# The first layer's down projection as seven half-size products, with the weight sums computed in both layers

## The chip, the cores and the metric

One NeuronCore of a Trainium2 chip runs the whole kernel. The metric is the device time of one execution in microseconds (us), as the median of several executions. The engines are named as the profile names them: PE (TensorE, matmuls) with PEld (its weight loads), DVE (VectorE), ACT (ScalarE), POOL (GpSimd) and SP (SyncE, which only issues DMAs here).

## The reference

A decoder trunk of two layers over 512 tokens of width 1024, all float32. Each layer has a token mixer of three branches (an RWKV-7 recurrence, chunked retention, a spatial gate), merged by gates and added to `x`, and then a gated MLP with a causal convolution of width 3:

```
for l in range(DEPTH):                                  # DEPTH = 2
    h = rmsnorm(x, norm1_g[l])
    p = h @ w_in[l]
    ...                                                 # three branches, gates
    x = x + jnp.sum(gates * proj, axis=2) @ w_out[l]
    x = x + conv_ffn(rmsnorm(x, norm2_g[l]), ffn_w_up[l], ffn_conv_w[l], ffn_conv_b[l], ffn_w_down[l])
return rmsnorm(x, final_g)

def conv_ffn(h, w_up, conv_w, conv_b, w_down):
    u = h @ w_up                                        # 1024 -> 2 * 2816
    ...                                                 # causal conv of width 3
    gate, val = jnp.split(c, 2, axis=-1)
    return (jax.nn.silu(gate) * val) @ w_down           # 2816 -> 1024
```

The change concerns the last product, `(silu(gate) * val) @ w_down`: 2816 rows of weights are 22 blocks of 128, or 11 pairs of blocks, and there are 1024 output features and 512 tokens.

## The kernel before

**Products.** To keep float32 precision every matrix product is done as three passes (`mm3`, L146): both operands are split into a high part rounded to the matmul's format and the low remainder, and high x low, high x high and low x high are accumulated. A block of weights of 128 x 512 elements is called a unit. `unit` (L81) hands out units in the order in which they are used and keeps a few loaded and split ahead: `load` (L122) issues the DMA on SP, `part` (L131) makes the high part on ACT (L140) and the low part on DVE (L141). `AHEAD` says how many units are split ahead for each kind of stage.

**Layout.** Within a layer activations stand with features on the partitions and tokens along the free dimension. `act` is the MLP's inner activation.

**The up projection** (`ffn_up`, L1090) has 44 columns of 128 outputs: 22 gate columns (index `i`) and the value column that belongs to each. One column is two units, 24 matmuls of 128x512. For each column DVE multiplies by the norm's factor (`fu`, L1120), ACT starts the convolution (`cv`, L1122), DVE adds its other two taps (L1123, L1124); for each `i` ACT and DVE make the gated product `fth` (L1128, L1129). In the first layer each `fth` is then split (L1131). In the second layer two neighbours are combined by `halves` (L1140): four DVE operations on 128x256 halves, three DMAs to DRAM on POOL's queue, and two splits.

**The down projection of the first layer** (`ffn_down`, L1158) is plain: for each of 8 blocks of outputs `m`, 22 x 3 matmuls of 128x512 over `act`, with weights from `wdn`; then `x[m]` is updated (L1164), normalised for the next layer, squared, and stored by POOL (L1168).

**The down projection of the second layer** (`last`, L1173) is done by a scheme of Strassen's kind: each pair of weight blocks (256 rows) with the two halves of the outputs makes a 2 x 2 block matrix, the tokens' halves likewise, and seven products of half the size replace eight. Four of the seven weight operands are sums and differences of the raw blocks. They don't depend on the activations, and `presum` (L246) computes them early: four loads of raw blocks on POOL's queue (L262), four DVE operations of 128x512 (L251 to L254), four stores to DRAM on POOL's queue (L257). The table `PRE` (L27) places the 11 pairs: four in the first layer's up projection (at `i` = 2, 4, 6, 8), seven in the first layer's down projection (one for each `m` from 0 to 6).

**The recurrence** (`rwkv`, from L703) runs over 8 chunks `c` of 64 tokens. Its small matmuls wait for DVE and ACT (`xb`, printed as XB, L717; `U`, L731; the state `St`, printed as S, L742 and L743); while they wait, PE works at units of other projections (`fill`), with weights as `wh`, `wl` in three buffers. After every second chunk the output `y` is normalised (a power on POOL, L762), transposed on DVE (`yt`) and sent through DRAM and back (`turned`, L233: one store `tr`, four loads `yF`), on SP's queue.

**The norm between the layers** (`norm_bcast`, L285) sums the squares over the partitions by two 128x512 matmuls with a matrix of ones (L290, L291), inside the first columns of the next stage (`firstF`, L320).

DVE, ACT and POOL execute in the order in which their instructions stand. `keep_in_program_order` (`po`, `kept`) pins an instruction to its place among the other pinned ones of its engine; the rest is placed by a scheduler when the program is built.

## Time and profile before

| | |
|---|---|
| three executions | 1694.98, 1695.05, 1697.68 us; median 1695.05 |
| profiled execution | 1692.75 us; its span 1691.0 us, 1.75 us lie around it |
| granted TensorE clock | 0.999 |
| first layer: up projection, down projection | about 505 to 734 us, 734 to 853 us |
| second layer: up projection, down projection | about 1347 to 1583 us, 1583 to 1685 us |
| recurrences (8 chunks) | about 210 to 300 us, 1056 to 1145 us |
| POOL queue: `pre<-wdt` loads, `ts<-pre` stores | 44 of each, 256 KB each |
| SP queue: `wr<-wall`, `wr<-wdn`, `wr<-wdt`, `wr<-ts` | 480, 48 (8 of them half-size), 33, 44 |

The profile shows one execution, engine by engine. A group row gives a source line, its engine, its operation, its shapes and its count, with the busy time and the mean duration of one. Matmuls are pipelined: their durations overlap (a 128x512 matmul shows 390 ns), so what a matmul costs is read from the distance between the starts of two that follow each other. "Idle before" names what an engine waited for ahead of an instruction.

### The profile page before, as it was taken

What the parts mean: (1) busy time and instruction counts of PE and PEld (TensorE: products, weight loads), DVE (VectorE), ACT (ScalarE), POOL (GpSimd) and SP (SyncE); (2) the same over time, 40 slices, a digit from 0 to 9 for tenths busy, and PEclk for the clock granted to TensorE, in tenths of its full rate; (3) what the DMA queues carried; (4) which work ended last, traced back from release to release, by engine and by line L of the source; (5) the groups of instructions that cost most, each with busy time, mean ns of one, the idle gap of its engine ahead of it and who ended that gap; (6) DMA issues with size and microseconds to landing.
All of it is one profiled execution on the core that took longest, in us unless ns stands there. A gap on an engine that the chain in (4) does not pass through costs nothing.

```text
span 1691.0 us, 27937 instructions
## 1 busy us (share of the span) xinstructions
PE 1682.8 (100%) x10247; PEld 1382.6 (82%) x10247; DVE 1216.5 (72%) x2115; ACT 794.1 (47%) x1365; POOL 261.3 (15%) x376
## 2 busy tenths in 40 slices
PE   9999999999999999999999999999999999999998
PEld 7888877888888888888888888778888888888887
DVE  7887745578669877665568888465786688887877
ACT  6563533554255444433346544335542544444565
POOL 1121000303301200003321210003032012210000
PEclk9999999999999999999999999999999999999999
DMA  5236553625544533147743265536254424443775
GB/s 183 88 111 203 179 176 98 189 84 163 191 144 149 194 124 95 63 146 263 250 147 96 92 206 187 176 100 188 84 163 166 152 98 144 142 140 110 242 247 178
DMA packets 143385, 260.01 MB, mean 154 GB/s; under 512 B 19440, under 2 KB 35440, under 8 KB 143248
## 3 DMA queue, kind: packets, MB, share of 16 engines
q1 hardware_dynamic: 117056, 188.41, 35.5%
q0 software_dynamic: 17552, 54.15, 9.7%
q10 hardware_dynamic: 8640, 15.67, 2.6%
q8 instruction: 80, 1.31, 0.3%
q14 instruction: 57, 0.47, 0.1%
HBM read 212.94 MB, written 45.22 MB: 153 GB/s over the span
## 4 chain that ended last, share of the span: by engine, by line
PE 99%; DVE 1%; ACT 0%; DMA 0%; issue 0%; DVEq 0%; ACTq 0%
PE acc L157 89%; PE sm L157 3%; PE sm L694 2%; PE sm L948 1%; PE sm L601 1%; PE sm L1056 0%; PE acc L359 0%; PE sm L564 0%; PE sm L563 0%; PE sm L976 0%; PE sm L1003 0%; PE sm L848 0%; PE acc L319 0%; PE sm L839 0%; DMA wr<-wall 0%; PE sm L618 0%
## 5 line engine op out<-in xcount | busy, mean ns | idle before, releaser
L157 PE MATMUL acc<-lo,sh 128*128 128x512 f32 x1108 | 432.1, 390 | 0.0
L157 PE MATMUL acc<-hi,sh 128*128 128x512 f32 x1108 | 432.0, 390 | 0.0
L157 PE MATMUL acc<-hi,sl 128*128 128x512 f32 x1108 | 425.0, 390 | 0.0
L140 ACT CAST sh<-wr 128x512 fp32r<-128x512 f32 (+1 forms) x375 | 226.4, 614 | 294.7 <-PE acc L157 165.7
L141 DVE TENSOR_TENSOR sl<-wr,sh 128x512 fp32r<-128x512 f32 (+1 forms) x375 | 253.0, 683 | 95.3 <-ACT sh L140 70.2
L141 DVE TENSOR_TENSOR wl<-wr,wh 128x512 fp32r<-128x512 f32 x238 | 167.9, 708 | 142.8 <-ACT wh L140 139.9
L140 ACT CAST wh<-wr 128x512 fp32r<-128x512 f32 x238 | 146.9, 619 | 247.6 <-PE acc L157 155.6
L157 PEld LDWEIGHTS acc<-hi,sl 128*128 128x128 f32 x1108 | 208.0, 188 | 43.8 <-DVE gth L1071 0.3
L157 PEld LDWEIGHTS acc<-lo,sh 128*128 128x128 f32 x1108 | 208.1, 188 | 43.7 <-issue 0.9
L157 PEld LDWEIGHTS acc<-hi,sh 128*128 128x128 f32 x1108 | 208.0, 188 | 43.2 <-issue 0.3
L157 PE MATMUL acc<-lo,wh 128*128 128x512 f32 x584 | 230.1, 394 | 0.1
L157 PE MATMUL acc<-hi,wl 128*128 128x512 f32 x584 | 228.3, 391 | 0.0
L157 PE MATMUL acc<-hi,wh 128*128 128x512 f32 x584 | 227.7, 390 | 0.0
L1122 ACT ACTIVATE cv<-fu,pc 128x512 f32<-128x512 f32 x88 | 71.7, 816 | 139.4 <-DVE fu L1120 139.2
L157 PEld LDWEIGHTS acc<-hi,wl 128*128 128x128 f32 x584 | 109.6, 188 | 24.1 <-issue 0.9
L157 PEld LDWEIGHTS acc<-lo,wh 128*128 128x128 f32 x584 | 109.6, 188 | 23.8 <-DVE rwp L523 0.5
L157 PEld LDWEIGHTS acc<-hi,wh 128*128 128x128 f32 x584 | 109.7, 188 | 22.3 <-issue 0.2
L157 PE MATMUL acc<-ah,sh 128*128 128x512 f32 x352 | 108.3, 389 | 0.0
L1123 DVE SCALAR_TENSOR_TENSOR cv<-fu,pc,cv 128x511 f32<-128x511 f32 x88 | 65.8, 749 | 34.3 <-ACT cv L1122 34.3
L157 PE MATMUL acc<-wl,hi 128*128 128x512 f32 x212 | 85.8, 405 | 0.0
L1120 DVE TENSOR_TENSOR fu<-acc,rsF 128x512 f32<-128x512 f32 x88 | 60.3, 685 | 32.5 <-PE acc L157 31.5
L157 PE MATMUL acc<-wh,hi 128*128 128x512 f32 x212 | 82.5, 389 | 0.0
(368 smaller groups left out, 2452.5 us busy)
## 6 DMA issues: line engine op xcount, KB each, us to landing
wr<-wall SPq DMA_DIRECT2D x480, 256.0 KB, 2.9
gd<-gth ACTq DMA_DIRECT2D x48, 256.0 KB, 3.3
gth<-gd POOLq DMA_DIRECT2D x48, 256.0 KB, 3.3
pre<-wdt POOLq DMA_DIRECT2D x44, 256.0 KB, 6.0
ts<-pre POOLq DMA_DIRECT2D x44, 256.0 KB, 3.0
wr<-ts SPq DMA_DIRECT2D x44, 256.0 KB, 4.0
wr<-wdn SPq DMA_DIRECT2D x40, 256.0 KB, 3.7
wr<-wdt SPq DMA_DIRECT2D x33, 256.0 KB, 3.8
```

The lines of the kernel that those rows point to most:

```text
L140: self.kept(self.nc.scalar.copy(hi[:, :n], raw[:, :n]))
L141: self.kept(self.nc.vector.tensor_tensor(lo[:, :n], raw[:, :n], hi[:, :n], op=SUB))
L157: i = self.nc.tensor.matmul(*x, **y, **kw)
L601: i = T.matmul(pK[hv[1 - h], j, :], bk[hv[h], c, 1, :], x[hv[h], c, :], start=True, stop=True)
L694: po(T.matmul(o, l, r, start=start, stop=True, skip_group_check=True))
L948: po(T.matmul(X[h][:, i, :], lhsT, rhs, start=new[h], stop=stop, skip_group_check=True))
L1120: V.tensor_tensor(u, ps, self.rsF, op=MUL)
L1122: A.activation(t, u, AF.Identity, scale=self.p("cw2", j), bias=self.p("cb", j))
L1123: V.scalar_tensor_tensor(t[:, 1:], u[:, :511], self.p("cw1", j), t[:, 1:], op0=MUL, op1=ADD)
```

## The change

1. `ffn_down` uses seven products of half the size, as `last` does, but keeps features on the partitions: a unit of weights is 128 x 512 (half of the outputs), and each product multiplies 4 blocks of 128 outputs with 256 tokens. That is 11 pairs x 7 products x 4 blocks x 3 passes = 924 matmuls of 128x256, in place of 8 x 22 x 3 = 528 of 128x512. The code that both layers share moves to `kit` and `half`. Weights of both layers now come from `wdt` and the sums; `wdn` is gone.
2. `ffn_up` calls `halves` in the first layer too, and pins its order there from the third `i` on.
3. The weight sums are needed for both layers, and each layer makes its own: `sums_rw` makes four pairs (`RWS`) inside the layer's recurrence, in chunks 2 to 7, `sums` makes the other seven inside its up projection, one DVE operation ahead of each column for `i` from 3 to 16 (`UPS`). All these DVE operations and DMAs are pinned.
4. `norm_bcast` is replaced between the layers by `norm_stats` and `norm_rows`, which the first layer already used at its start: four 128x1 matmuls on the plain sum of squares, a power on POOL, four 128x128 transposes, a copy. They stand two half columns apart.
5. In the recurrence `xb` and `St` are pinned, and the trip of `y` through DRAM goes to POOL's queue.

```diff
-PRE = {(0, "f", 2): 0, (0, "f", 4): 1, (0, "f", 6): 2, (0, "f", 8): 3, (0, "d", 0): 4, (0, "d", 1): 5, (0, "d", 2): 6, (0, "d", 3): 7,
-       (0, "d", 4): 8, (0, "d", 5): 9, (0, "d", 6): 10}
+RWS, RWB, UPS = 4, (2, 4, 5, 6), range(3, 17)
-AHEAD = {None: 2, "p": 4, "r": 3, "f": 3, "u": 5, "q": 4}
+AHEAD = {None: 2, "p": 4, "r": 3, "f": 3, "u": 5, "q": 4, "k": 5, "w": 3}
...
+    def summed(self, l, q, b, p):
+        po = self.tc.keep_in_program_order
+        o, x, op = {7: (3, 1, SUB), 5: (1, 0, SUB), 6: (0, 3, ADD), 4: (2, 0, SUB)}[p]
+        po(self.nc.vector.tensor_tensor(b[o], b[o], b[x], op=op))
+        self.tsum[l, q, p] = self.dp.tile([128, 512], F32, name=self.nm("ts"))
+        po(self.nc.gpsimd.dma_start(self.tsum[l, q, p], b[o]))
...
+    def sums_rw(self, l):
...
+        first, b = [tile(0, 3, 1)], tile(0, 0, 2)
+        first.append(tile(1, 3, 1))
+        yield
+        for q in range(RWS):
+            b.update(first.pop(0))
+            self.summed(l, q, b, 7)
+            if q and q < RWS - 1:
+                first.append(tile(q + 1, 3, 1))
+            yield
+            for p in (5, 6, 4):
+                self.summed(l, q, b, p)
+            if q < RWS - 1:
+                b = tile(q + 1, 0, 2)
+            yield
+
+    def sums(self, l):
...
+        for q in range(RWS, NFF // 2):
+            n = get(q + 1) if q < NFF // 2 - 1 else None
+            for p in (7, 5, 6, 4):
+                self.summed(l, q, b, p)
+                yield
+            b = n
...
-                self.norm_bcast(st, l and ids[0] == 12)
+                self.norm_stats(st) if ids[0] == FIRST[0] else self.norm_bcast(st)
+            elif i == at + 2 and ids[0] == FIRST[0]:
+                self.norm_rows()
...
-            V.tensor_copy(xb, Q[:, 1])
+            po(V.tensor_copy(xb, Q[:, 1]))
+            self.presum(c - 1 in RWB)
...
-                    V.tensor_tensor(St, St, Q[:, 0], op=ADD)
+                    po(V.tensor_tensor(St, St, Q[:, 0], op=ADD))
                     po(V.tensor_tensor(St, St, f, op=MUL))
+                self.presum(c == 1 or c in RWB)
...
-            self.turned(o, self.r(n="yt"), y, nc.sync)
+            self.turned(o, self.r(n="yt"), y, nc.gpsimd)
...
-            self.keep = l == L - 1 and i > 1
+            self.keep = i > 1
             for j in (i, NFF + i):
+                self.presum(i in UPS)
...
-            if l < L - 1:
-                act.append(self.split(th, at))
-            elif i % 2 == 0:
+            if i % 2 == 0:
...
     def ffn_down(self, l, act, x, st):
-        for m in range(8):
-            ps = self.acc()
-            self.matF(ps, ("wdn", l, m, 0), act)
-            V.scalar_tensor_tensor(x[m], ps, 0.5, x[m], op0=MUL, op1=ADD)
+        def prod(ps, x, at, w, first, end, ms=range(4)):
+            for m in ms:
+                c = slice(128 * m, 128 * m + 128)
+                self.mm3(ps[m // 2][:, H[m % 2]], (w[0][:, c], w[1][:, c]), (x[0][:, at:at + 256], x[1][:, at:at + 256]),
+                         first and m % 2 == 0, end, skip_group_check=True)
...
+        for q in range(Q):
+            s, t = act[q][:2]
+            for p in (7, 5, 6, 4) if q < Q - 1 else (6, 7, 5, 4):
+                w = unit(p, q)
+                side(n)
+                n += 1
+                xs, at = {7: (t, 0), 5: (s, 0), 6: (s, 256), 4: (t, 256)}[p]
+                prod(pss[p], xs, at, w, q == 0, q == Q - 1)
...
+        for q in range(Q):
+            w = unit(1, q)
+            rest(q)
+            prod(out[1], ab[q], 0, w, False, q == Q - 1)
...
+        for q in range(Q):
+            w = unit(2, q)
+            prod(out[2], ab[q], 256, w, q == 0, q == Q - 1)
...
+        for q in range(Q - KEPT):
+            w = unit(3, q)
+            prod(out[3], s4[q // 2], q % 2 * 256, w, q == 0, False)
...
```

What moves is shown at three places. Line numbers of the changed program are its own (L140 and L156 there are L141 and L157 before). The first is PE where the first layer's down projection stands; `acc` is the accumulator in PSUM, behind the arrow stand the moving operand (`ah`, the split inner activation) and the weights. Before, this is a block of 128 outputs, here the head of the second of eight, which has 66 such rows:

```order
L157 MATMUL acc_1628_7673<-ah_1149_5568,sh_1612_7610 128x512
L157 MATMUL acc_1628_7673<-ah_1148_5567,sh_1612_7610 128x512
L157 MATMUL acc_1628_7673<-ah_1148_5567,sl_1613_7611 128x512
L157 MATMUL acc_1628_7673<-ah_1163_5624,sh_1612_7610 128x512
L157 MATMUL acc_1628_7673<-ah_1162_5623,sh_1612_7610 128x512
L157 MATMUL acc_1628_7673<-ah_1162_5623,sl_1613_7611 128x512
```

In the changed program this is the head of the first product, and such rows go on through 77 units of weights:

```order
L156 MATMUL acc_1694_7813<-ah_1186_5736,wh_1668_7706 128x256
L156 MATMUL acc_1694_7813<-ah_1185_5735,wh_1668_7706 128x256
L156 MATMUL acc_1694_7813<-ah_1185_5735,wl_1669_7707 128x256
L156 MATMUL acc_1694_7813<-ah_1186_5736,wh_1668_7706 128x256
L156 MATMUL acc_1694_7813<-ah_1185_5735,wh_1668_7706 128x256
L156 MATMUL acc_1694_7813<-ah_1185_5735,wl_1669_7707 128x256
L156 MATMUL acc_1695_7814<-ah_1186_5736,wh_1668_7706 128x256
```

A row after has half the tokens of a row before, and one unit of weights now serves 12 rows in a run, with four blocks of outputs side by side in two accumulators. The 528 rows of 128x512 (the first block among the last rows of the up projection) become 924 of 128x256. Outside of this stage PE's order is the same but for item 4 and for one fill unit in each layer that stands 45 rows earlier or later.

The second place is DVE at the last chunk (`c` = 7) of the first layer's recurrence; `wl` are the low parts of fill units, `ro` and `rb` belong to the rotary embedding. Before:

```order
L717 COPY XB_98_397<-sm_617_3329 128x256
L916 TENSOR_TENSOR ro_624_3422<-ro_624_3422,rb__625_3423 128x8x32
L141 TENSOR_TENSOR wl_632_3485<-wr_621_3404,wh_631_3484 128x512
L911 TENSOR_TENSOR ro_633_3500<-qs_589_3161,tab_577_3080 128x512
L912 TENSOR_TENSOR rb__634_3501<-qs_589_3161,tab_578_3081 128x8x32
L141 TENSOR_TENSOR wl_644_3539<-wr_627_3444,wh_643_3538 128x512
L753 TENSOR_REDUCE s1_635_3514<-y_607_3267 128x8
```

After, with the sums of the fourth pair (`cs` are their raw blocks, two blocks to a tile):

```order
L749 COPY XB_98_397<-sm_637_3389 128x256
L950 TENSOR_TENSOR ro_645_3485<-ro_645_3485,rb__646_3486 128x8x32
L140 TENSOR_TENSOR wl_656_3557<-wr_642_3467,wh_655_3556 128x512
L945 TENSOR_TENSOR ro_657_3572<-qs_603_3203,tab_585_3104 128x512
L946 TENSOR_TENSOR rb__658_3573<-qs_603_3203,tab_586_3105 128x8x32
L249 TENSOR_TENSOR cs_615_3289<-cs_615_3289,cs_631_3364 128x512
L140 TENSOR_TENSOR wl_668_3611<-wr_651_3516,wh_667_3610 128x512
L249 TENSOR_TENSOR cs_631_3364<-cs_631_3364,cs_615_3289 128x512
L249 TENSOR_TENSOR cs_631_3364<-cs_631_3364 128x512
L787 TENSOR_REDUCE s1_659_3586<-y_623_3315 128x8
```

A sum that reads `cs_631` now stands ahead of the fill unit's low part `wl_668`. The third place is POOL over chunks 5 to 7 of the same recurrence. Before it held two powers of the norm of `y` and then the trips of the rotary tiles:

```order
L762 TENSOR_TENSOR rs8_559_2957<-s2_558_2954,con_78 128x8
L762 TENSOR_TENSOR rs8_603_3255<-s2_602_3252,con_78 128x8
L243 DMA tr_700_3814<-qkt_699_3812 128x512
L239 DMA qkT_698_3811<-tr_700_3814 32x4x128 x4
L243 DMA tr_703_3823<-qkt_702_3821 128x512
```

After, the second of these powers is followed by the trip of `y` and the stores (`ts`) and loads of the sums:

```order
L251 DMA ts_614_3287<-cs_588_3129 128x512
L256 DMA cs_615_3289<-wdt 128x512 x2
L796 TENSOR_TENSOR rs8_619_3303<-s2_618_3300,con_78 128x8
L242 DMA tr_622_3309<-yt_621_3307 128x512
L238 DMA yF_620_3306<-tr_622_3309 32x4x128 x4
L251 DMA ts_628_3356<-cs_588_3129 128x512
L251 DMA ts_629_3359<-cs_596_3179 128x512
L251 DMA ts_630_3362<-cs_596_3179 128x512
L256 DMA cs_631_3364<-wdt 128x512 x2
```

The load of `cs_631` stands behind the four loads `yF`, which wait for the landing of `tr_622`, which waits for DVE's transpose of `y`.

More of the change, by code (lines that the diff above doesn't have):

```diff
@@ L265, in norm_new, with get, presum @@
+    def sums(self, l):
+        def get(q):
+            b = {i: self.f(n="pre") for i in (3, 1, 0, 2)}
+            self.raw4(l, q, b)
+            return b
+        b = get(RWS)
+        yield
[3 more added lines that the diff above has]
+                self.summed(l, q, b, p)
+                yield
+            b = n
+    def presum(self, ok=True):
+        if ok:
+            next(self.sum, None)
     def norm_new(self):
@@ L1102, in ffn_up @@
         first = self.firstF(l, (78, 79, 80), st, 3)
-        if l == 0:
-            self.fpre = [[self.f(n="pre") for _ in range(4)] for _ in range(4)]
+        self.sum = self.sums(l)
+        self.presum()
         for i in range(NFF):
-            if l == 0 and i % 2 == 0 and 2 <= i <= 10:
-                self.presum(l, "f", i)
             if x and i % 2 == 1 and i < 17:
@@ L1171, in ffn_down @@
+        self.pin = self.keep = False
         return x, xd
```

173 lines of the change are left out of this document (102 added, 71 removed).

## The prediction

> **What bounds the kernel now.** I read the page's busy times first, then its chain of work that ended last.
>
> ```profile
> PE 1682.8 (100%) x10247; PEld 1382.6 (82%) x10247; DVE 1216.5 (72%) x2115; ACT 794.1 (47%) x1365; POOL 261.3 (15%) x376
> ...
> PEclk9999999999999999999999999999999999999999
> ...
> PE 99%; DVE 1%; ACT 0%; DMA 0%; issue 0%; DVEq 0%; ACTq 0%
> ```
>
> PE is busy for 1682.8 of 1691.0 us at a granted clock of 0.9 or more in every slice, and the chain is PE's own work for 99%. So only fewer or cheaper PE rows can shorten the program, and everything that the change lays on other engines costs nothing until PE has to wait for it. The second view is a table of stretches: the first layer's up and down projection, the end of its recurrence, the second layer's up and down projection.
>
> ```profile
> core 0: us, PE busy (x) PEld busy (x) DVE busy (x) ACT busy (x) POOL busy (x), PEclk, DMA share, GB/s
> 505.00:745.00 240.00, 240.00 (x1060) 198.77 (x1060) 185.50 (x285) 114.19 (x176) 15.03 (x28) 1.00 0.38 123
> 745.00:865.00 120.00, 120.00 (x532) 99.36 (x530) 63.28 (x100) 40.37 (x69) 34.31 (x64) 1.00 0.73 242
> 200.00:300.00 100.00, 99.78 (x1416) 77.85 (x1415) 50.78 (x100) 40.63 (x78) 7.23 (x7) 1.00 0.45 139
> 1347.00:1583.00 236.00, 236.00 (x1043) 195.45 (x1042) 193.57 (x309) 106.40 (x174) 38.36 (x70) 1.00 0.41 131
> 1583.00:1685.00 102.00, 102.00 (x480) 85.09 (x478) 79.34 (x158) 60.35 (x115) 4.33 (x8) 1.00 0.71 235
> ```
>
> PE has no idle time in either projection and 0.22 us in 100 of the recurrence. DVE is loose in the down projection (63 of 120 us), tighter in the last stage (79 of 102), and nearest to its limit in the up projections.
>
> **The down projection.** The cost of a matmul is the distance between starts. The first two rows are the ends of a run of 47 rows of 128x512 in the last stage, the other two of a run of 36 rows of 128x256.
>
> ```profile
> 1659.68 0.39 PE L157 MATMUL acc<-sh,hi 128*128 128x512 f32 x1
> ...
> 1670.11 0.39 PE L157 MATMUL acc<-wh,lo 128*128 128x512 f32 x1
> ...
> 1680.78 0.28 PE L157 MATMUL acc<-sl,hi 128*128 128x256 f32 x1
> ...
> 1684.98 0.28 PE L157 MATMUL sm<-sh,lo 128*128 128x256 f32 x1
> ```
>
> 10.43 us over 46 distances is 226.7 ns; 4.20 us over 35 is 120.0 ns. Half the columns cost 53% and not 50%. Removed are 528 x 226.7 = 119.7 us, added 924 x 120.0 = 110.9 us: **-8.8 us**, and not the eighth (15.0 us) that seven products for eight promise.
>
> A weight load stands before every matmul, and the page shows 1382.6 us for 10247 of them, 135 ns each, longer than this pace. The 36 rows at 120.0 ns have such loads as well, so the loads stay hidden at half size. The Trainium skill ("TensorE: Matmul & The Clock Gate", section "Back-to-back issue gap") speaks against the change: it gives a sustained spacing of load and matmul of 81 ns for 128 columns and 131 ns for 512. A line between the two gives, as an estimate from that page, 98 ns for 256, hence 528 x 131 = 69.2 us removed and 924 x 98 = 90.6 us added, and a sum of +23.7 us for the change where mine is below. The trace disagrees with it (226.7 and 120.0 ns here), so the measurement decides.
>
> Is the stage fed? It takes 77 units of weights in about 111 us, 1.44 us each (12 x 120.0 ns). The last stage takes units of the same size and kind at 12 x 0.1133 = 1.36 us at 235 GB/s and with PE busy for 102.00 of 102.00 us. I cost the feeding at nothing; without that cover it is rival E. In product 2 and at the start and end of the stage the DVE operations on the results (12 to 16 of 128x256) stand ahead of low parts of weights, which the rows don't show in this form: between 0 and some 3 us (16 x 0.42 less 3 units ahead x 1.44), and I take **+0.5**, near to the last stage, which has the same form and no wait.
>
> **The norm.** Two 128x512 matmuls of the norm go; four 128x1 matmuls and four transposes come.
>
> ```profile
> L272 PE MATMUL sm<-con,sq x8: 164/250/251, 21.9 to 22.6; 128*128 128x1 f32 x8
> L281 PE MATMUL sm<-con,rs x4: 271/272/273, 25.6 to 25.9; 128*128 128x128 f32 x4
> L276 POOL TENSOR_TENSOR rs<-ms,con x1: 1032/1032/1032, 24.1 to 24.1; 128x4 f32<-128x4 f32 x1
> ```
>
> From first start to the last end the eight passes take 0.7 + 0.25 = 0.9 us, the transposes 0.3 + 0.27 = 0.6 us; pipelined into matmuls I take 0.8 and 0.45. Two matmuls of 226.7 ns are 0.45. **+0.8 us**. The power on POOL between them takes 1.0 us and lies under the 24 matmuls of a column (5.4 us).
>
> **The up projections.** PE needs 96 x 226.7 ns = 21.76 us for four columns of outputs (two gate and value pairs). What DVE needs in that time decides whether anything is lost.
>
> ```profile
> 1421.94 0.68 DVE L141 TENSOR_TENSOR sl<-wr,sh 128x512 fp32r<-128x512 f32 x1
> 1422.54 0.68 DVE L1120 TENSOR_TENSOR fu<-acc,rsF 128x512 f32<-128x512 f32 x1
> 1423.14 0.68 DVE L141 TENSOR_TENSOR sl<-wr,sh 128x512 fp32r<-128x512 f32 x1
> 1424.11 0.75 DVE L1123 SCALAR_TENSOR_TENSOR cv<-fu,pc,cv 128x511 f32<-128x511 f32 x1 [0.29 <-ACT cv L1122]
> 1424.90 0.75 DVE L1124 SCALAR_TENSOR_TENSOR cv<-fu,pc,cv 128x510 f32<-128x510 f32 x1
> 1425.57 1.46 DVE L141 TENSOR_TENSOR sl<-wr,sh 128x512 fp32r<-128x512 f32 x2
> 1427.63 0.69 DVE L1120 TENSOR_TENSOR fu<-acc,rsF 128x512 f32<-128x512 f32 x1 [0.60 <-PE acc L157]
> 1429.20 0.75 DVE L1123 SCALAR_TENSOR_TENSOR cv<-fu,pc,cv 128x511 f32<-128x511 f32 x1 [0.89 <-ACT cv L1122]
> ```
>
> An operation on halves:
>
> ```profile
> L1154 DVE TENSOR_TENSOR fth<-fth 128x256 f32<-128x256 f32 x11 | 4.7, 424 | 1.2 <-DMA ab<-fth 0.8
> ```
>
> A full-width operation holds DVE for 0.60 us (starts 1421.94, 1422.54, 1423.14), the two taps of the convolution for 0.79 and 0.67 (1424.11, 1424.90, 1425.57), 0.73 on average, an operation on halves for 0.4. In the second layer four columns have after the change 8 low parts of weights, 4 `fu`, 4 sums, 2 `fth`, 2 splits and 1 transpose, 21 x 0.605 = 12.7 us; 8 taps, 5.8 us; 4 operations on halves, 1.6 us: 20.1 us. In the first layer, without the transpose, 19.5. So 1.6 and 2.2 us of every 21.76 are left. A second reading agrees:
>
> ```profile
> 520.00:560.00 40.00, 36.23 (x58) 1.00 0.56 179
> 1410.00:1450.00 40.00, 34.31 (x56) 1.00 0.46 144
> ```
>
> These are DVE's busy times alone, first layer and second, before the change. The first stretch already holds sums at the rate of one a column, and PE loses nothing in it. The change adds 1.6 us of `halves` to four columns there, 2.9 us in 40, and 4 sums (2.4 us, 4.4 in 40) in the second: 39.2 and 38.8. Shown times overlap by some 0.08 an operation, so about 36 are truly taken. Where `fu` is directly followed by its tap, DVE waits 0.89 for ACT; the order after puts another operation between the two in most places. I take **0**; the bound on the other side is rival B. Weights split three units ahead, 3 x 12 x 226.7 ns = 8.2 us, carry short delays.
>
> **The recurrences.** Sixteen sums a layer come to a DVE that is half idle (50.78 of 100 us), but they are pinned between operations for which PE waits, and one chain crosses POOL's queue. These two rows of DVE belong to the last two chunks of the first layer:
>
> ```profile
> 284.55 0.71 DVE L236 STREAM_TRANSPOSE yt<-y 128x512 f32<-128x512 f32 x1
> ...
> 297.56 0.69 DVE L141 TENSOR_TENSOR wl<-wr,wh 128x512 fp32r<-128x512 f32 x1 [2.40 <-ACT wh L140]
> ```
>
> This row of PE reads the second of them:
>
> ```profile
> 302.98 0.39 PE L157 MATMUL acc<-wl,hi 128*128 128x512 f32 x1
> ```
>
> A trip through DRAM on POOL's queue takes this long, store and then the four loads that wait for it:
>
> ```profile
> 302.29 0.61 POOL L243 DMA_DIRECT2D tr<-qkt  x1 [19.18 <-DVE qkt L236]
> 306.51 2.21 POOL L239 DMA_DIRECT2D qkT<-tr  x4 [3.62 <-DMA tr<-qkt]
> ```
>
> The low part that starts at 297.56 is done at 298.25, 4.7 us ahead of PE. After the change a sum that reads `cs_631` stands ahead of it. The load of `cs_631` waits on POOL for the whole trip of `y`: transpose done at 285.26, with four sums put ahead of it (2.4 us, of which I count 1.0 as falling into idle time of DVE) 286.7; store and its landing 4.2 us (302.29 to 306.51), 290.9; four loads issued in 2.2, 293.1; the store out of the same buffer 3.0 to land, 296.1; the load itself 3.9 to 7.2, by these rows of the page and of the loads' own line:
>
> ```profile
> ts<-pre POOLq DMA_DIRECT2D x44, 256.0 KB, 3.0
> ```
>
> ```profile
> L262 POOL DMA_DIRECT2D pre<-wdt x44: 536/538/543, 452.6 to 842.2; - x44
> ...
> DMA to landing us min/median/max: 3.9/6.0/7.2
> ```
>
> That is 300.0 to 303.3, and with the sum and the low part (1.3) 301.4 to 304.6, or up to 306.8 if the two loads go one behind the other. Against 302.98 PE waits between 0 and 3.8 us. Nothing can be gained there, since PE has only 0.2 us of idle time. I take 0.5 in each layer, near to the early end, as the trips of the sums have no other traffic on POOL: **+1.0 us**. The sum:
>
> -8.8 + 0.8 + 0.5 + 0 + 1.0 = **-6.5 us**. On the profiled execution's 1692.75 this gives 1686.25 us; that execution lay 2.3 us below the median of the runs, 1695.05, so the forecast on the median is **1688.5 us**.
>
> **Rivals.** B: **DVE becomes the bound of the up projections.** If all four waits of `fu` for ACT in four columns are exposed (4 x 0.89 = 3.6), DVE needs 23.7 us in the second layer and 23.1 in the first, 1.9 and 1.3 above 21.76. Over seven such groups a layer that is 13.6 + 9.4 = 23.0 us, less up to 8.2 a layer of weights split ahead: +6.6 to +23.0, 1695 to 1711 us, in the middle 1703, slower than before. It decides from a group above 21.76 us. For it speaks that the operations are pinned; against it, 36.23 of 40 us without a loss.
>
> C: **the recurrence waits.** The late end of the chain above, 3.8 us in each layer in place of 0.5: 1688.5 + 6.6 = 1695.1, no change; smaller waits of `xb` and the state, which the sums delay too, come on top. For it speaks that the margins are 4.7 us and less.
>
> D: **a half-size matmul costs exactly half** (113.3 ns), -15.0 in place of -8.8: 1682.3. The 36 rows speak against it.
>
> E: **the down projection isn't fed**: 77 units, some of them sums just written, at 240 GB/s and more. If half of the units come 0.15 us late, 5.8 us are lost: 1694. The last stage speaks against it.
>
> F: **the weight load sets the pace** of the half-size matmuls. From 129.5 ns (119.7 / 924) on the stage loses; at the load's 135 ns it takes 124.7 us, 13.8 more than at 120.0: 1702 us. The 36 rows at 120.0 speak against it. The rule of the Trainium skill above lies on this side.
>
> **How the numbers follow.** The forecast A has 0.60, with a range of its own from 1685 to 1691.6 (without the two small waits 1687, with the norm at nothing 1686, with 3 us of waits more 1691.5). B has 0.15, C 0.14, D 0.03, E 0.07, F 0.01. About 0.2%, 3.4 us, is what a measurement of this kernel can tell from no change, so faster ends at 1691.7 and slower begins at 1698.4. Faster: A and D, 0.63. Same: C 0.10, B 0.05, E 0.05, 0.20. Slower: B 0.10, C 0.04, E 0.02, F 0.01, 0.17. The range from 1683.5 to 1699 leaves out D, most of B and the upper ends of C and E, some 0.18.
>
> **What would show it.** Right: rows of 128x256 in the first down projection 120 ns apart, that stage about 111 us long, PE still busy for all of the up projections. Wrong, and how: PE waiting for `sl` in the up projections with DVE above 95% of a stretch (B); PE waiting for `wl` just after the last chunk, with POOL's load of `cs` behind the trip of `y` (C); PE waiting for weights in the down projection (E); a distance other than 120 ns (D, F).

## The result and the profile after

The changed kernel took 1714.68 us (median of 4 runs, 1710.77 to 1716.93) against 1695.01 us before: a ratio of 1.0111, 95% interval 1.0088 to 1.0135. It is slower by 1.1%, some 20 us; the forecast was 1688.5. The profiled execution took 1713.43 us, its span is 1711.4. Two lines of its page:

```profile
PE 1684.9 (98%) x10653; PEld 1395.8 (82%) x10653; DVE 1288.0 (75%) x2279; ACT 814.1 (48%) x1412; POOL 353.1 (21%) x534
...
PE 62%; issue 6%; DMA 5%; DVE 5%; ACT 1%; POOL 1%; SPq 0%; DVEq 0%; ACTq 0%; POOLq 0%
```

The chain was PE's own work for 99%, and is so for 62% now; transfers, DVE and issuing have come in. The same kinds of stretches as before (first recurrence with its end, first up and down projection, second recurrence, second up projection, last stage):

```profile
core 0: us, PE busy (x) PEld busy (x) DVE busy (x) ACT busy (x) POOL busy (x), PEclk, DMA share, GB/s
200.00:330.00 130.00, 122.24 (x1509) 95.16 (x1507) 73.50 (x141) 47.45 (x92) 43.09 (x68) 1.00 0.64 201
505.00:742.00 237.00, 236.27 (x1042) 195.08 (x1042) 203.51 (x331) 107.95 (x175) 44.63 (x83) 1.00 0.52 170
744.00:858.00 114.00, 113.54 (x935) 112.75 (x934) 87.18 (x164) 63.21 (x112) 4.48 (x8) 1.00 0.70 230
1056.00:1180.00 124.00, 118.67 (x1367) 92.50 (x1366) 69.88 (x135) 45.85 (x88) 43.46 (x68) 0.99 0.64 203
1360.00:1600.00 240.00, 237.24 (x1036) 193.27 (x1035) 205.54 (x336) 107.06 (x173) 66.68 (x123) 1.00 0.57 186
1600.00:1705.00 105.00, 103.55 (x484) 85.86 (x483) 80.85 (x160) 61.79 (x119) 4.33 (x8) 1.00 0.70 229
```

PE stands still for 7.8 us in the first recurrence, 5.3 in the second, 2.8 in the second up projection, 1.5 in the last stage, 0.7 and 0.5 in the first up and down projection. Before, the recurrence stretch had 0.2. What PE waited for, by the view of its waits (us in all, times, longest):

```profile
PE acc L156 <- DVE wl L140: 6.7, 6, 1.9
PE sm L725 <- DVE S L776: 3.2, 4, 1.4
PE acc L156 <- ACT sh L139: 2.4, 4, 0.7
PE sm L725 <- ACT U L764: 2.3, 1, 2.3
PE sm L725 <- DVE XB L749: 1.5, 2, 0.9
...
PE acc L156 <- DVE sl L140: 1.1, 2, 0.7
```

These are not single large waits but some twenty small ones; the largest, 2.3 us, stands at 234 us. A wait costs more than the idle time shown, since a matmul's modelled end lies behind the start of the next. Here is one of the second recurrence, with two of the rows behind it:

```profile
1165.39 0.39 PE L156 MATMUL acc<-wh,lo 128*128 128x512 f32 x1
1167.70 0.50 PE L156 MATMUL acc<-wl,hi 128*128 128x512 f32 x1 [1.92 <-DVE wl L140]
...
1169.11 0.63 PE L156 MATMUL acc<-wh,hi 128*128 128x512 f32 x1
1169.54 0.63 PE L156 MATMUL acc<-wh,lo 128*128 128x512 f32 x1
```

The first two rows start 2.31 us apart, where 0.23 is usual: 2.08 us were lost, and 1.92 are shown. The wait has a second price. From 1168.27 to 1171.67 eight distances take 3.40 us in place of 1.81, and the granted clock is lower there:

```profile
core 0: us, PE busy (x), PEclk, DMA share, GB/s
1165.00:1170.00 5.00, 3.08 (x11) 0.83 0.57 189
1170.00:1175.00 5.00, 5.00 (x20) 0.83 0.85 254
```

That is another 1.6 us. Not every wait has such a stretch behind it: after the one of 2.3 us at 234 the rows keep their usual distance. The sum is read more surely from the starts of the same matmul in both traces:

| PE's matmul | before | after | late by |
|---|---|---|---|
| ahead of the first recurrence | 196.71 | 198.44 | 1.7 |
| product with the state, last chunk (`c` = 7) | 289.19 | 295.78 | 6.6 |
| bias of the spatial gate, after the recurrence | 353.30 | 364.00 | 10.7 |
| begin of the second layer | 883.81 | 888.80 | 5.0 |
| product with the state, second recurrence | 1134.72 | 1142.58 | 7.9 |
| bias of the spatial gate, second layer | 1198.83 | 1211.60 | 12.8 |
| last matmul | 1684.98 | 1705.23 | 20.3 |

The recurrences cost 9.0 and 7.8 us, the second up projection and last stage 7.5. Between 364 and 889 us the changed kernel gains 5.7.

### The profile page after: what moved, and what is told of

Its sections match the earlier page's. It is cut to its first block, busy times and chain, and to the rows that moved or that the text cites. A ratio compares the mean times of both kernels' runs of the same rounds, so it can differ in the third digit from the quotient of the medians.

```text
span 1711.4 us, 29320 instructions
## 1 busy us (share of the span) xinstructions
PE 1684.9 (98%) x10653; PEld 1395.8 (82%) x10653; DVE 1288.0 (75%) x2279; ACT 814.1 (48%) x1412; POOL 353.1 (21%) x534
## 4 chain that ended last, share of the span: by engine, by line
PE 62%; issue 6%; DMA 5%; DVE 5%; ACT 1%; POOL 1%; SPq 0%; DVEq 0%; ACTq 0%; POOLq 0%
PE acc L156 53%; PE sm L156 5%; DMA wr<-wall 2%; DVE sl L140 1%; PE sm L982 1%; DMA ts<-cs 1%; PE sm L725 1%; DVE cv L1156 1%; DMA s<-wl 1%; DVE wl L140 1%; DMA ws<-sgw 1%; DMA tr<-bkT 1%; DVE fu L1153 0%; ACT cv L1155 0%; PE sm L1090 0%
## 5 line engine op out<-in xcount | busy, mean ns | idle before, releaser
L156 PE MATMUL acc<-lo,sh 128*128 128x512 f32 (+1 forms) x1156 | 446.6, 387 | 2.5 <-ACT sh L139 2.4
L156 PE MATMUL acc<-hi,sh 128*128 128x512 f32 (+1 forms) x1156 | 445.6, 385 | 0.0
L156 PE MATMUL acc<-hi,sl 128*128 128x512 f32 (+1 forms) x1156 | 432.9, 386 | 1.0 <-DVE sl L140 0.7
L139 ACT CAST sh<-wr 128x512 fp32r<-128x512 f32 x361 | 217.9, 616 | 225.9 <-DMA wr<-wall 102.6
L140 DVE TENSOR_TENSOR wl<-wr,wh 128x512 fp32r<-128x512 f32 x281 | 196.9, 705 | 143.1 <-ACT wh L139 130.3
L140 DVE TENSOR_TENSOR sl<-wr,sh 128x512 fp32r<-128x512 f32 x361 | 245.1, 690 | 75.7 <-ACT sh L139 69.8
L156 PEld LDWEIGHTS acc<-lo,sh 128*128 128x128 f32 x1156 | 217.2, 188 | 49.3 <-ACT sh L139 5.7
L156 PEld LDWEIGHTS acc<-hi,sl 128*128 128x128 f32 x1156 | 217.2, 188 | 46.2 <-DVE sl L140 2.7
L156 PEld LDWEIGHTS acc<-hi,sh 128*128 128x128 f32 x1156 | 217.3, 188 | 43.1 <-issue 0.3
L156 PE MATMUL acc<-lo,wh 128*128 128x512 f32 (+1 forms) x624 | 241.7, 387 | 0.0
L156 PE MATMUL acc<-hi,wl 128*128 128x512 f32 (+1 forms) x624 | 239.6, 384 | 0.1
L156 PE MATMUL acc<-hi,wh 128*128 128x512 f32 (+1 forms) x624 | 239.1, 383 | 0.0
L156 PEld LDWEIGHTS acc<-hi,wl 128*128 128x128 f32 x624 | 117.3, 188 | 24.9 <-DVE wl L140 1.1
L156 PEld LDWEIGHTS acc<-lo,wh 128*128 128x128 f32 x624 | 117.3, 188 | 23.7 <-DVE rwp L554 0.3
L156 PEld LDWEIGHTS acc<-hi,wh 128*128 128x128 f32 x624 | 117.4, 188 | 22.3 <-issue 0.2
L156 PE MATMUL acc<-wl,hi 128*128 128x512 f32 x212 | 87.0, 411 | 5.9 <-DVE wl L140 5.9
L1156 DVE SCALAR_TENSOR_TENSOR cv<-fu,pc,cv 128x511 f32<-128x511 f32 x88 | 65.9, 749 | 26.6 <-ACT cv L1155 26.1
L156 PE MATMUL acc<-wh,lo 128*128 128x512 f32 x212 | 83.2, 392 | 0.0
L156 PE MATMUL acc<-wh,hi 128*128 128x512 f32 x212 | 83.0, 391 | 0.0
L1157 DVE SCALAR_TENSOR_TENSOR cv<-fu,pc,cv 128x510 f32<-128x510 f32 x88 | 65.7, 748 | 2.1
```

The source lines that it names most:

```text
L139: self.kept(self.nc.scalar.copy(hi[:, :n], raw[:, :n]))
L140: self.kept(self.nc.vector.tensor_tensor(lo[:, :n], raw[:, :n], hi[:, :n], op=SUB))
L156: i = self.nc.tensor.matmul(*x, **y, **kw)
L1156: V.scalar_tensor_tensor(t[:, 1:], u[:, :511], self.p("cw1", j), t[:, 1:], op0=MUL, op1=ADD)
L1157: V.scalar_tensor_tensor(t[:, 2:], u[:, :510], self.p("cw0", j), t[:, 2:], op0=MUL, op1=ADD)
```

## The experiments

All times are medians, with the ratio to the kernel before in the same runs; 0.2% is the limit of what is told apart. Line numbers of a variant can lie one off those of the changed kernel.

**Is it the sums at all?** The first run leaves every weight sum out.

```diff
-        self.sum = self.sums_rw(l)
+        self.sum = iter(())
...
-        self.sum = self.sums(l)
+        self.sum = iter(())
...
-            if p > 3:
+            if 0:
                 return self.unit("tsum", l, (q, p), 0)
-            return self.unit("wdt", l, 2 * q + (p > 1), 512 * (p == 3))
+            return self.unit("wdt", l, 2 * q + (p in (2, 3, 6, 7)), 512 * (p in (3, 5, 7)))
```

> The changed kernel without any weight sums: the four products that should read sums read raw blocks of weights instead (its result is therefore not the reference's), with the same loads on SP; the 88 DVE operations, 88 loads and 88 stores of the sums on POOL's queue are gone. Everything else of the change stays (seven half-size products, the halves in both layers, the norm by transposes, the trip of y on POOL). Theory 1, the sums make PE wait (about 16 us in the two recurrences, 5 in the second up projection): 1687 to 1693 us, about what the forecast had for the whole change. Rival, the time is lost by the rest (halves in the first layer, the trip on POOL's queue, the new norm, the down projection's feed): 1705 us or more.

1688.06 us, ratio 0.9966 (0.9956 to 0.9976): 6.3 us faster than before. The seven products, the halves in the first layer, the new norm and the trip on POOL give together what the forecast had for them (without its +1.0 for the recurrences it is 1687.5); all that went wrong is the price of the sums, 26.6 us.

**Which sums?** The same edit for the recurrences alone (with `if p > 3 and q >= RWS`), and for the up projections alone (with `if 3 < p and q < RWS`).

> The changed kernel without the 16 sums of each recurrence (their products read raw blocks; the result is not the reference's); the sums in the up projections stay. Theory 1: the recurrences' stalls go, 12 to 16 us less than the changed kernel, 1699 to 1703 us, and PE has no waits above 0.5 us between 210 and 325 us. Rival, the trip of y on POOL and DVE's pins alone cost the recurrence its time: within 3 us of the changed kernel, 1711 to 1717.

1694.89 us, ratio 1.0005 (0.9996 to 1.0015). The recurrences' sums cost 19.8 us, more than was expected.

> The changed kernel without the 28 sums of each up projection (their products read raw blocks; the result is not the reference's); the sums in the recurrences stay. Theory 1: only the waits of the second layer's up projection go, 4 to 7 us less than the changed kernel, 1708 to 1711 us. If the up projections were the main cause (rival B of the forecast): 1695 to 1702.

1704.08 us, ratio 1.0058 (1.0037 to 1.0079), 10.6 us less than with them, also more than expected. Taken singly the two prices make 30.4, together 26.6. The second price is the less sure one: the four times of this run lie between 1699.46 and 1708.57. Where the recurrences hold no sums, the up projections' sums cost 6.8 (1694.89 against 1688.06).

**The trip on POOL's queue.** The fourth run moves only the trip of `y` back.

```diff
-            self.turned(o, self.r(n="yt"), y, nc.gpsimd)
+            self.turned(o, self.r(n="yt"), y, nc.sync)
```

> The changed kernel with the trip of y back on SP's queue, all sums kept. If the chain of the forecast's rival C (loads of raw blocks behind the trip on POOL) makes the waits at the end of each recurrence: the last chunk's waits of wl go, 3 to 6 us less, 1708 to 1712 us. If the waits come from DVE's order and from shared DMA transfers: within 2 us of the changed kernel, 1713 to 1717. If the trip then holds up SP's weight loads: slower than 1717.

1701.62 us, ratio 1.0043 (1.0028 to 1.0058): 13.1 us less, over twice what was expected. In the changed kernel's trace this is the chain, DVE first:

```profile
292.62 0.71 DVE L235 STREAM_TRANSPOSE yt<-y 128x512 f32<-128x512 f32 x1
...
306.94 0.69 DVE L249 TENSOR_TENSOR cs<-cs,cs 128x512 f32<-128x512 f32 x1 [5.21 <-DMA cs<-wdt]
307.55 0.69 DVE L140 TENSOR_TENSOR wl<-wr,wh 128x512 fp32r<-128x512 f32 x1
...
320.33 0.69 DVE L459 TENSOR_TENSOR ws<-ws,con 128x512 f32<-128x512 f32 x1 [3.49 <-DMA ws<-sgw]
```

and POOL's queue between the two:

```profile
293.63 0.61 POOL L242 DMA_DIRECT2D tr<-yt  x1 [1.77 <-DVE yt L235]
297.43 2.20 POOL L238 DMA_DIRECT2D yF<-tr  x4 [3.19 <-DMA wr<-wall]
299.62 1.64 POOL L251 DMA_DIRECT2D ts<-cs  x3
302.34 1.07 POOL L256 DMA_DIRECT2D cs<-wdt  x2 [1.07 <-DMA ts<-cs]
...
316.08 0.54 POOL L242 DMA_DIRECT2D tr<-qkt  x1 [5.68 <-PE acc L156]
```

The store of `y`, the wait for its landing (the four loads read what it wrote, though the row names a weight load), the four loads, three stores of sums and then the loads of the last pair: DVE stands for 5.2 us before a sum, and the weights' low part behind it is late. The backlog goes on after that: POOL's first trip of `qkt` is issued at 316.08, 13.8 us later than the same trip before (302.29), where PE was late by 6.6 us at the last chunk, ahead of it. PE loses 0.60, 0.85 and 1.76 us by these at 308, 317 and 322, and 4.1 by the table's starts.

**Is it the trip's place, or the loads behind it?** Here the trip stays on POOL; the fourth pair goes to the up projections, and no load of raw blocks is left behind the third trip.

```diff
-RWS, RWB, UPS = 4, (2, 4, 5, 6), range(3, 17)
+RWS, RWB, UPS = 3, (2, 4, 5), range(3, 19)
```

> The changed kernel with the trip of y still on POOL's queue, but three pairs in each recurrence, behind chunks 2, 4 and 5, so that no load of raw blocks stands behind the third trip; the fourth pair moves to the up projections. A true kernel. If the loads behind the trip make the end of the recurrences late: DVE no longer waits for a load near 307 us, the waits of wl near 308, 317, 322, 1155 and 1168 us go, and the time is 1705 to 1709 us. If the trip's place on POOL's queue is enough: 1712 us or more with these waits.

1699.21 us, ratio 1.0032 (1.0022 to 1.0042), 15.5 less than the changed kernel and some 6 below the expectation's lower end, and the waits named are gone. DVE at the same place waits for no transfer:

```profile
302.60 0.69 DVE L140 TENSOR_TENSOR wl<-wr,wh 128x512 fp32r<-128x512 f32 x1 [2.40 <-ACT wh L139]
305.47 0.69 DVE L787 TENSOR_REDUCE s<-y 128x8 f32<-128x512 f32 x1 [2.18 <-ACT y L781]
```

The trip on POOL is harmless without the pair (here), and the pair without the trip (the run before). So it is the two together: the load queued behind the trip, under a DVE operation that stands ahead of others. In the traces the bias of the spatial gate starts at 358.7 and 1199.3 us here, 5.3 and 12.3 earlier than in the changed kernel, so most of the gain lies ahead of it.

**What is left in the recurrences with the trip on SP: DVE's time or the transfers?** The fifth run drops the sums' DVE operations in the recurrences (`if q >= RWS:` ahead of the operation in `summed`); the sixth keeps them on three tiles loaded once and drops the rest of the loads and the stores.

> On the variant with the trip of y on SP's queue (1701.6 us): in the recurrences the loads and stores of the sums stay, their 16 DVE operations a layer are left out (raw blocks are stored in place of sums; the result is not the reference's). There PE waits 8.5 us in the two recurrences. Theory D, DVE's time makes these waits, by operations ahead of the state's update and by keeping POOL's power of the norm of y from running: 1694 to 1697 us, and the longest POOL power is under 2.2 us, not 3.6. Rival M, the transfers make them, by slowing the trips on SP's queue: 1699 us or more.

1710.42 us, ratio 1.0090 (1.0075 to 1.0105): slower than with the DVE operations, by 8.8 us. That lies in rival M's range, but neither theory gave a reason for more than 1701.6. The longest POOL power is 2.18 us, as theory D had said. Without operations to wait for, POOL issues the stores as soon as raw blocks have landed, in a block with the loads of the rotary tables, and SP's weight loads are late. POOL and DVE of this run:

```profile
240.37 2.21 POOL L252 DMA_DIRECT2D ts<-cs  x4
245.35 1.07 POOL L257 DMA_DIRECT2D cs<-wdt  x2 [2.78 <-DMA ts<-cs]
246.41 2.22 POOL L932 DMA_DIRECT2D tab<-rot  x4
```

```profile
261.69 0.69 DVE L140 TENSOR_TENSOR wl<-wr,wh 128x512 fp32r<-128x512 f32 x1 [9.25 <-ACT wh L139]
262.30 0.42 DVE L776 TENSOR_TENSOR S<-S,sm 128x256 f32<-128x256 f32 x1
```

The state's update stands on DVE behind the low part of a fill unit, whose weights have not come; PE waits 4.7 us for the state at 263 and 5.4 at 1112. The waits of 1.4 us near 294 and 1138 are gone. All waits of this trace together are 4.7 us more than in the variant with the trip on SP alone (18.5 against 13.8), about half of what was lost. The rest is the clock behind the two long waits:

```profile
263.32 1.13 PE L726 MATMUL sm<-S,X 64*64 64x64 f32 x32 [4.67 <-DVE S L777]
...
265.40 0.63 PE L156 MATMUL acc<-wh,lo 128*128 128x512 f32 x1
265.83 0.63 PE L156 MATMUL acc<-wl,hi 128*128 128x512 f32 x1
```

These rows stand 0.43 us apart, and the granted clock is 0.58 from 265 to 270 us. Against the usual distances the two stretches (here and at 1112) lose some 4.4 us, an estimate from their starts.

> On the variant with the trip of y on SP's queue (1701.6 us): in the recurrences the 16 DVE operations a layer stay, on three tiles that are loaded once; all other loads and all stores of these sums are left out, and their products read raw blocks (the result is not the reference's). Theory D: 1698 to 1702 us with the same waits for the state S. Rival M: 1693 to 1696 us. Both to about half: 1696 to 1698.

1702.78 us, ratio 1.0051 (1.0034 to 1.0068), no different from 1701.62 within the noise, as theory D had it. It keeps just those two waits of 1.35 us, and 2.3 and 2.1 at 232 and 1061, where the three tiles' first loads stand. Each half alone makes waits, at places of its own; the price isn't the sum of two halves.

**The wait near 294.** The seventh run puts three pairs behind even chunks only, on the variant with the trip on SP.

```diff
-RWS, RWB, UPS = 4, (2, 4, 5, 6), range(3, 17)
+RWS, RWB, UPS = 3, (2, 4, 6), range(3, 19)
...
```

> On the variant with the trip of y on SP's queue (1701.6 us): three pairs of sums in each recurrence, only behind chunks 2, 4 and 6, so that none stands between the output y of an odd chunk and its power on POOL; the fourth pair moves to the up projections (two more groups of four columns each). A true kernel, result as the reference's. If the sums ahead of that power make the waits of 1.4 us for the state: the waits near 294 and 1138 us go, and with a quarter less of the sums 1697 to 1700 us. If the up projections pay for the fourth pair: 1702 us or more.

1698.53 us, ratio 1.0023 (1.0013 to 1.0032), as expected, and the two waits are gone. Behind them is POOL's power of the norm of `y`. In the changed kernel, POOL and then DVE:

```profile
288.29 3.57 POOL L796 TENSOR_TENSOR rs<-s,con 128x8 f32<-128x8 f32 x1 [2.82 <-DVE s L794]
```

```profile
289.92 0.42 DVE L950 TENSOR_TENSOR ro<-ro,rb__636_3386 128x256 f32<-128x256 f32 x1
291.90 0.69 DVE L797 TENSOR_TENSOR y<-y,rs 128x512 f32<-128x512 f32 x1 [1.56 <-POOL rs L796]
```

The power takes 3.57 us in place of 1.7. DVE works without a pause until 290.34, and the power ends 1.5 us after that, which is nearly its whole usual time, as if it ran only once DVE was still. DVE then waits for it, in order, ahead of the state's update. All eight powers of the changed kernel and of this run (shortest, median, longest, in ns):

```profile
L796 POOL TENSOR_TENSOR rs<-s,con x8: 1667/1707/3577, 240.6 to 1162.4; 128x8 f32<-128x8 f32 x8
```

```profile
L796 POOL TENSOR_TENSOR rs<-s,con x8: 1662/1667/1921, 236.2 to 1154.4; 128x8 f32<-128x8 f32 x8
```

The Trainium skill ("SBUF — State Buffer", section "SBUF: two separate sides") has it that a DVE operation with two inputs in SBUF takes a port pair that GpSimd needs, that whichever starts first gets it, and that the loser is blocked and not slowed. The traces agree for POOL. The sums have two such inputs, and so have the operations around them. A power that begins while such an operation runs ends 1.5 us after DVE is through: it takes 1.74 us with 0.20 of the operation left, 2.21 with 0.68 (the variant with the trip on SP, 314.79 us), 3.57 with 2.05 us of operations without a pause. Powers that begin ahead of a DVE operation take 1.63 to 1.68. Once, in the run without the fourth pair (1129.26 us), a power took 1.97 with the same 2.05 us of operations ahead, as if it had got in between two of them. The other way round little shows: a DVE operation that begins under a running power is longer by less than 0.1 us.

What stays in this run are waits of 2.8 us at 259 and 1.4 at 1100, which the kernels with the trip on POOL don't have. At the first SP issues the loads of the trip 8.6 us after its store (6.1 before), and weight loads stand behind them; at the second that gap is 7.9, no longer than before (8.2). So their cause stays open.

**The second up projection: DVE's time or the transfers?** Two halves again, on the variant with the trip on SP: without the sums' DVE operations, and without their transfers.

```diff
-        po(self.nc.vector.tensor_tensor(b[o], b[o], b[x], op=op))
+        if q < RWS:
+            po(self.nc.vector.tensor_tensor(b[o], b[o], b[x], op=op))
...
```

> On the variant with the trip of y on SP's queue (1701.6 us): in the up projections the loads and stores of the sums stay, their 28 DVE operations a layer are left out (raw blocks are stored; the result is not the reference's). If DVE's time makes the waits of the second layer's up projection (rival B of the forecast): 1696 to 1698 us. If late weight loads make them, because the transfers of the sums share the DMA engines: within 1.5 us of 1701.6.

1702.08 us, ratio 1.0037 (1.0024 to 1.0050): nothing won. PE's waits in the second up projection:

```profile
PE acc L156 <- ACT sh L139: 2.3, 3, 1.4
PE acc L156 <- DVE wl L140: 1.1, 1, 1.1
PE sm L156 <- DVE wl L140: 0.5, 1, 0.5
```

> On the variant with the trip on SP's queue (1701.6 us): in the up projections the 28 DVE operations of the sums a layer stay, on tiles that are loaded once; all other loads and all stores of these sums are left out, and their products read raw blocks (the result is not the reference's). If the transfers make the weight loads late: the second up projection keeps waits of under 1 us in all, 1695 to 1698 us. If DVE's time alone is enough to make waits: 1700 to 1703, with waits for DVE's low part instead of ACT's high part.

1698.51 us, ratio 1.0024 (1.0014 to 1.0033), 3 us less, half a us above what was expected of the transfers. The intervals of the two times touch, so the waits are the better evidence. The variant with the trip on SP had this one, and here it is gone:

```profile
PE acc L156 <- ACT sh L139: 1.6, 3, 0.7
```

```profile
PE sm L156 <- DVE wl L140: 0.2, 1, 0.2
PE acc L156 <- DVE wl L140: 0.2, 1, 0.2
```

DVE is as busy in this stretch as in the changed kernel (207.23 of 235 us against 205.54 of 240). So it is the transfers that make these waits. The landing times of the weight loads between 1360 and 1600 us, first in the run without any sums, then in the changed kernel, then in this run:

```profile
DMA to landing us min/median/max: 2.4/3.1/5.8
```

```profile
DMA to landing us min/median/max: 2.5/3.4/8.1
```

```profile
DMA to landing us min/median/max: 2.4/3.0/5.6
```

In the variant with the trip on SP they are 2.5, 3.5 and 7.9. The median hardly moves; the latest load comes after 8.1 us, and 8.2 us is all that three units split ahead are worth, with the split still to follow.

**Ways to make the sums cheaper.** Three runs, all with the trip on SP; the edits are shown against the changed kernel. The first, with three pairs behind even chunks, loads a raw block ahead of each sum instead of four in a row, and the other two keep that:

```diff
...
-            n = get(q + 1) if q < NFF // 2 - 1 else None
-            for p in (7, 5, 6, 4):
+            n = {}
+            for p, i in zip((7, 5, 6, 4), (3, 1, 0, 2)):
+                if q < NFF // 2 - 1:
+                    n[i] = self.f(n="pre")
+                    self.raw4(l, q + 1, {i: n[i]})
                 self.summed(l, q, b, p)
...
```

> The variant with the trip on SP's queue and three pairs behind even chunks (1698.5 us), and in the up projections one raw block of the next pair is loaded ahead of each sum in place of four in a row. A true kernel. If bursts of four loads make the weights of the second up projection late (weight loads that land after 7.2 us beside them and after 2.6 to 3.5 otherwise): the waits for ACT's high part there go, 1695 to 1697 us. If the mean rate of the transfers counts, not the burst: 1698 to 1700.

1701.13 us, ratio 1.0041 (1.0028 to 1.0054), 0.2% above the run with even chunks, which lacks only this edit, and above both expectations. The weight loads land as late as there (median 3.6, longest 7.2 us, against 3.5 and 7.8), and PE still waits 2.2 us for ACT's high part. Blocks of four loads are not the cause; the theory of bursts falls for the up projections.

> As the run before, with two pairs in each recurrence, behind chunks 4 and 6, their first loads issued behind chunk 3 and not ahead of the chunks, and nine pairs in the up projections from their second pair of columns on. A true kernel. If the six early loads slow the trips of chunks 0 to 2 on SP's queue: the waits near 230 and 1060 us (1.1 and 0.6) go, and those near 259 and 1100 us (2.8 and 1.4) get smaller: 1692 to 1695 us. If the up projections cannot take two more pairs: 1697 us or more.

```diff
-RWS, RWB, UPS = 4, (2, 4, 5, 6), range(3, 17)
+RWS, RWB, UPS = 2, (4, 6), range(1, 19)
...
-                self.presum(c == 1 or c in RWB)
+                self.presum(c == 3 or c in RWB)
...
```

1702.24 us, ratio 1.0047 (1.0031 to 1.0062). The waits near 230 and 1060 are gone, as expected of later first loads; of the other two, the one near 259 shrank to 1.1 us and the one near 1100 grew to 2.3. The second up projection now waits 6.7 us, 4.2 of them for DVE's low part: with nine pairs it is DVE as well.

> No sums in the recurrences: all 11 pairs of a layer from the third block of the output projection ahead of the up projection to its 19th pair of columns, one sum and one load of a raw block a column; the trip of y on SP's queue. A true kernel. If the sums cost PE time only where they stand beside latency-bound chunks and in bursts: no waits in the recurrences and at most 3 us in the up projections, 1688 to 1692 us, below the kernel before (1694 to 1695). If an up projection with all the sums runs out of DVE time or of transfers: 1696 us or more.

```diff
-RWS, RWB, UPS = 4, (2, 4, 5, 6), range(3, 17)
+RWS, RWB, UPS = 0, (), range(19)
...
+        self.sum = self.sums(l)
+        self.presum()
         for m in range(8):
+            self.presum(m > 1)
             xi = self.u(n="xi")
...
```

1711.19 us, ratio 1.0101 (1.0084 to 1.0117). The recurrences have no wait above 0.25 us, but the output projection and the first columns behind it wait 6.7 us for `xi`, which stands on DVE behind the sums, and in the second up projection PE waits another 4.8 us for the two parts of its weights, twice what it does in the changed kernel. The hoped-for time was wrong by some 20 us; the other reading, that such a stage runs out of DVE time or of transfers, came true.

No version here beats the kernel before; the nearest are the one with three pairs behind even chunks, 0.23% slower, and the one without the fourth pair, 0.32% slower.

## Why the prediction was wrong, point by point

- **The down projection, -8.8 us: right.** These two rows of the changed kernel have 72 distances of 128x256 between them, 8.63 us, 119.9 ns each:

```profile
790.00 0.28 PE L156 MATMUL sm<-ah,wl 128*128 128x256 f32 x1
...
798.63 0.28 PE L156 MATMUL acc<-ah,wl 128*128 128x256 f32 x1
```

  The stage was fed, with 0.5 us of idle time in 114, so the +0.5 for its starts was right too; rivals D, E and F fall. The +0.8 of the norm was not measured alone. The three terms make -7.5; the run without sums has -6.3, with an interval from -4.1 to -7.5.
- **The up projections, 0: nearly right in the first layer (0.7 us idle), wrong in the second (2.8 us idle).** The step asked only whether DVE has the time, and DVE had it: 205.54 of 240 us, 86%, below the 95% that rival B asked for, and B's waits for DVE's low part were not what came. It gave the 28 loads and 28 stores a layer no price. Leaving out these transfers removed the waits; leaving out DVE's part did not.
- **The recurrences, +1.0: this is the step that failed. The term was taken for one small wait in each layer, and the sums there cost 19.8 us.** The chain over POOL's queue was there as told, and even its length was right: from the end of the transpose at 293.3 to the landing at 306.9 are 13.6 us, where the prediction had 13.3 to 16.6. But it was priced as one late low part against one slack of 4.7 us. At that place PE lost just 0.60. What stands behind the waiting sum on DVE, and behind the loads on POOL, was not followed: the last pair with that trip cost 13 to 15 us. Two more kinds of waits were not priced at all: DVE's time that keeps POOL's power from running (1.4 us in each layer), and the first loads beside the trips of the first chunks (2.3 us at 234, 0.9 at 1066). Nor was the slower clock behind a wait (1.6 us at 1168).
- **Rival C had the place and the mechanism, and at most about half of the size.** Its worst case was the top of one wait in each layer, 7.6 us in all against the 13 to 15 of that chain. A stage in which each engine's order is pinned does not have one slack: a delay moves everything that is due behind it.
- **The reasons for the low end looked at the wrong thing.** A DVE that is half idle was set against the sixteen sums, and 0.5 us a layer was taken because the trips of the sums have no other traffic on POOL. For the length of the chain that was right, as it came out at its early end. In engines that wait for each other in turn it says nothing of what the delay moves; the slack of each instruction behind it does.

## What to carry to other kernels

Moving work to idle engines is free only if nothing with a due time stands behind it in the same order: follow each new wait into the queues behind it (DVE's, POOL's, SP's), and not only to the instruction that waits. Give each added transfer a price where weight loads have a lead of a few units, since here the latest loads moved (5.8 to 8.1 us) and the median hardly did. Count with a wait as more than its idle time, since a stretch at a lower clock can follow it. And test the parts apart: without the sums the change was worth what its matmuls said, which no view of the whole run shows.

## What the runs showed of the hardware that was not expected

- A small power on POOL took 3.57 us instead of 1.66 while DVE ran operations on two inputs without a pause, and ended 1.5 us after the last of them.
- Behind some waits of PE, of 1.9, 2.3, 4.7 and 5.4 us, its matmuls of 128x512 stood 0.43 us apart in place of 0.23 for some 2 to 4 us (the changed kernel at 1168, the sixth run at 234, the fifth at 265 and 1113). The granted clock in slices of 5 us was 0.83, 0.78, 0.58 and 0.50 at the lowest. Behind another of 2.3 us (the changed kernel at 234) they did not. What decides it was not tried.
- An ACT copy stood behind the issue of a store that it does not need. In the changed kernel the copy of `U`, for which PE waits 2.3 us, stands behind the issue of a store on ACT's queue, 4.15 us after the store's data are ready at 229.61:

```profile
233.76 0.33 ACTq L508 DMA_DIRECT2D gd<-gth  x1
234.12 0.37 ACT L764 COPY U<-sm 128x256 f32<-128x256 f32 x1 [4.51 <-DMA wr<-wall]
```

  Before, the same copy stood for 1.55 us behind the same issue, within its slack. What the issue waits for is not shown: the row names a weight load, but so does the row of POOL at 297.43, which waits for the trip's own store.
- Transfers alone (the fifth run) were worse than transfers and DVE operations together, by 8.8 us. From 240 to 260 us they moved 321 GB/s in place of 261; that the operations had spaced the stores is the likely reason, not a tested one.
- The changed kernel's times scatter over 6 us, those of the run without sums over 4, of the kernel before over 3 to 6 in a series. In the changed kernel the mean granted clock goes with it: 0.998 in the two shorter executions (1710.77 and 1713.43 us), 0.996 and 0.995 in the longer ones (1715.94 and 1716.93). What else decides it is open.
